# Reciprocal roots of the first block's norms: from VectorE's queue to GpSimd's

## The chip, the cores and the metric

The kernel runs on one core of a Trainium2 chip. A core has five engines that run side by side, each with its own queue of instructions in a fixed order: TensorE (matrix products, PE in the profile), VectorE (DVE), ScalarE (ACT), GpSimd (POOL) and SyncE (SP, which here only issues transfers). They wait for one another by semaphores. An instruction that has to wait holds up all that stand behind it in its engine's queue. The metric is the time of one execution on the device in microseconds, the median of several runs.

## The reference, cut to what matters

Two blocks are computed one after the other on 256 tokens of width 1024. The change touches the first block alone. It has two layers; the first also carries 256 context tokens along. Each layer normalizes its input, scales and shifts it by a modulation vector, multiplies by a wide matrix, and feeds the parts of the product to four branches: latent attention, a convolution, a Fourier mixing and a spatial gating.

```python
def _rmsnorm(x, g):
    y = x * lax.rsqrt(jnp.mean(x * x, axis=-1, keepdims=True) + RMS_EPS)
    return y * g

def _layernorm(x, g, b):
    mu = jnp.mean(x, axis=-1, keepdims=True)
    var = jnp.mean(jnp.square(x - mu), axis=-1, keepdims=True)
    return (x - mu) * lax.rsqrt(var + LN_EPS) * g + b
...
h = _rmsnorm(x, p["norm_g"]) * (1.0 + scale) + shift    # input of a layer
c_q = _rmsnorm(q_part, p["q_norm_g"])                   # latent attention, queries
c_kv = _rmsnorm(kv_part, p["kv_norm_g"])                # latent attention, keys and values
v = _layernorm(v, p["sgu_ln_g"], p["sgu_ln_b"])         # spatial gating
y = silu(_layernorm(y, p["conv_ln_g"], p["conv_ln_b"])) # convolution
```

Each of these has one reciprocal square root for each token, so one column of 128 numbers for a tile of 128 tokens. The second block has norms too; theirs are not touched.

## The kernel before, in words

Tokens lie in four tiles of 128 (t = 0, 1 are the tokens, t = 2, 3 the context), on the 128 partitions. All large products are made in three matmuls from a rounded high part and a remainder of each operand (hi and lo, whi and wlo): ScalarE casts a weight tile to whi and VectorE subtracts to get wlo, for 1024 columns at a time. Weights stream from memory through a few buffers (raw). The names in the profile are those of the tiles.

The order of the work is written by a planner in Python, `Sched`. It keeps a clock for each engine and runs generators: `main(t)` for the matmuls of a tile, and side generators for everything else (`mla`, `sgu`, `conv`, `fourier`, `modulate`, ...). `S.dve`, `S.act` and `S.pool` emit one instruction on VectorE, ScalarE or GpSimd and add its planned cost to the clock; a `Chain` carries the planned time of a dependent sequence. Nothing of it is on the chip: it only decides in which order instructions are emitted. The framework behind it then sets buffers and waits, and can place instructions of one engine that are ready ahead of others.

What the change and the prediction's steps touch:

- `rsqrt` (L372): a first guess from the bits of the number and three Newton steps, tiles rs_y, rs_h and rs_t; for one column 8 instructions, for more columns 11. All on VectorE, line L221 of the helper `S.dve`.
- `modulate` (L1293): between the two layers, once for each of the four tiles. The squares come from ScalarE (junk, ss), then the sum rw, the root, then xn = x times the root, one half on ScalarE and one half on VectorE; TensorE transposes xn, ScalarE applies the modulation (f) and casts (hhi), VectorE makes the remainder (hlo).
- `layernorm` (L1324), called by `sgu` for four tiles in the first layer and two in the second: statistics (bn, mv), rwl, the root, the shift lnb, and then ln on ScalarE.
- `mla` (L1575): squares on ScalarE (jq, jk), the sum ssm with a small constant, the root of two columns (queries and keys) or of one (`kv_only`, tiles 2 and 3 in the second layer). ScalarE uses it when it copies the products pkv and pq out of PSUM (qkf, V).
- `conv` (L1419): 31 taps of two multiply-adds each on VectorE (acc), spread between other work, and then a root of four or two columns.
- GpSimd's queue holds memsets (qkf, qz) and a few transfers.

Of the kernel before, what the change touches and what calls it, by code (L numbers as in the profile page):

```python
# [10 lines left out]
I32 = mybir.dt.int32  # L11
AF = mybir.ActivationFunctionType
ALU = mybir.AluOpType
# [6 lines left out]
EPS = 1e-6  # L20
# [73 lines left out]
LN_EPS = 1e-5  # L94
# [72 lines left out]
class Sched:  # L167
# [51 lines left out]
    def dve(self, ch, n, fn, *a, x=0.0, **k):  # L219
        self.issue("dve", ch, 0.07 + n * 0.00104 + x)  # L220
        ins = getattr(self.nc.vector, fn)(*a, **k)  # L221
        return ins

    def pool(self, ch, cost, fn, *a, **k):
        self.issue("pool", ch, cost)
        return getattr(self.nc.gpsimd, fn)(*a, **k)
# [142 lines left out]

def rsqrt(S, ch, pool, w, n, tag):  # L372

    y = pool.tile([P, n], F32, tag=tag + "y", name="rs_y", bufs=4)
    h = pool.tile([P, n], F32, tag=tag + "h", name="rs_h")
    t = pool.tile([P, n], F32, tag=tag + "t", name="rs_t")
    S.dve(ch, n, "tensor_scalar", y.bitcast(I32), w.bitcast(I32), -0.5, float(0x5F3759DF), op0=ALU.mult, op1=ALU.add)
    S.dve(ch, n, "tensor_scalar", h, w, -0.5, None, op0=ALU.mult)
    for _ in range(3):
        if n == 1:  # L380
            S.dve(ch, n, "scalar_tensor_tensor", t, y, h, y, op0=ALU.mult, op1=ALU.mult, x=0.06)
        else:
            S.dve(ch, n, "tensor_tensor", t, y, y, op=ALU.mult)
            S.dve(ch, n, "tensor_tensor", t, t, h, op=ALU.mult)
        S.dve(ch, n, "scalar_tensor_tensor", y, t, 1.5, y, op0=ALU.add, op1=ALU.mult)
    return y


class Second:
# [8 lines left out]
    def open(self, apool, src):  # L398

        self.ap = apool  # L400
        tab = apool.tile([P, src.shape[1]], F32, name="tab")
        if PADS[1]:
            apool.tile([P, PADS[1] // 4], F32, name="pad2")
        self.nc.gpsimd.dma_start(tab, src)
# [563 lines left out]
class First:  # L968
# [192 lines left out]
    def start(self):  # L1161
# [3 lines left out]
        self.ada = [self.p1.tile([P, 24, 2], F32, name=f"ada{l}") for l in range(2)]  # L1165
        self.p1.tile([P, PADS[2] // 4], F32, name="pad1")
        self.cbc = [self.s4([P, 1024], f"cbc{s}") for s in both]
# [125 lines left out]
    def modulate(self, t, l, x, ch, ss, ev):  # L1293

        S, s = self.S, t // 2
        new = self.hp.tile if t < 2 else self.p1.tile
        kw = (dict(tag="hhi"), dict(tag="hlo")) if t < 2 else (dict(tag="s4", bufs=S4),) * 2
        hi, lo = (new([P, KT, P], F32R, name=n, **k) for n, k in zip(("hhi", "hlo"), kw))
        w = self.small.tile([P, 1], F32, tag="rw", name="rw")
        S.dve(ch, 1, "scalar_tensor_tensor", w, ss[:, 0:1], EPS, ss[:, 1:2], op0=ALU.add, op1=ALU.add)  # L1300
        r = rsqrt(S, ch, self.small, w, 1, "r")
        xn = [self.normed(Chain(ch.t), x, r, n, n == 1) for n in range(2)]
        yield ch
        for n in range(2):
            for p in (0, 1):
                yield self.adaev[l, p, n]
            tp = self.psum("tp", "tpx")
            ch = S.chain()
            for k in range(4):
                self.tr(ch, tp[:, k * P:(k + 1) * P], xn[n][:, k * P:(k + 1) * P])  # L1310
            f = self.w2([P, 4, P], "f")
            for k in range(4):
                c = 4 * n + k
                S.act(ch, 128, "activation", f[:, k, :], tp[:, k * P:(k + 1) * P], AF.Identity,
                      scale=self.ada[l][:, 8 + c, s:s + 1], bias=self.ada[l][:, c, s:s + 1], x=0.15)
            h = slice(4 * n, 4 * n + 4)
            S.act(ch, 512, "copy", hi[:, h, :], f)
            S.dve(ch, 512, "tensor_sub", lo[:, h, :], f, hi[:, h, :].bitcast(F32))
            if n == 0:
                S.done(ev, ch)  # L1320
        self.hs[t] = lambda k: (hi[:, k, :], lo[:, k, :])


    def layernorm(self, ch, src, n):  # L1324

        S = self.S
        st = self.small.tile([P, 6], F32, tag="bn", name="bn")
        mv = self.small.tile([P, 2], F32, tag="mv", name="mv", bufs=4)
        S.dve(ch, n, "bn_stats", st, src)
        S.dve(ch, 6, "bn_aggr", mv, st)  # L1330
        w = self.small.tile([P, 1], F32, tag="rw", name="rwl")
        S.dve(ch, 1, "tensor_scalar", w, mv[:, 1:2], LN_EPS, None, op0=ALU.add)
        r = rsqrt(S, ch, self.small, w, 1, "r")
        b = self.small.tile([P, 1], F32, tag="lnb", name="lnb", bufs=4)
        S.dve(ch, 1, "scalar_tensor_tensor", b, mv[:, 0:1], -1.0, r, op0=ALU.mult, op1=ALU.mult)
        z = self.w2([P, 256], "ln")
        S.act(ch, 256, "activation", z, src, AF.Identity, scale=r, bias=b, x=0.15)
        return z
# [80 lines left out]
    def conv(self, l, streams):  # L1419
        nc, S = self.nc, self.S  # L1420
        for s in streams:
            for i in range(2):
                yield self.L[l].ev["glu", 2 * s + i]
        n = len(streams)
        sl = slice(streams[0], streams[-1] + 1)
        acc = self.p1.tile([P, 2, n, 256], F32, tag="acc", name="acc", bufs=1)
        acc = [acc[:, c] for c in range(2)]
        chs = [S.chain(), S.chain()]
        for j in range(31):
            for c in range(2):  # L1430
                src = self.glu[:, c, sl, j:j + 256]
                w = self.cw[l][:, c * 31 + j:c * 31 + j + 1]
                if j == 0:
                    S.dve(chs[c], 256 * n, "tensor_scalar", acc[c], src, w, self.col(l, "conv_b", c), op0=ALU.mult,
                          op1=ALU.add, x=0.12)
                else:
                    S.dve(chs[c], 256 * n, "scalar_tensor_tensor", acc[c], src, w, acc[c], op0=ALU.mult, op1=ALU.add, x=0.06)
            yield max(0.1, S.backlog("dve", 1.3) - CONV)
        ch = S.chain(*chs)
        yield ch  # L1440

        m = 2 * n
        mv = self.small.tile([P, 4, 2], F32, tag="mv4", name="mv4", bufs=1)[:, :m, :]
        ch, src = S.chain(), []
        for s in range(n):
            tp = self.psum(("tp", "ps")[s], "tpc")
            cs = S.chain()
            for i in range(2):
                for c in range(2):
                    self.tr(cs, tp[:, (2 * i + c) * P:(2 * i + c + 1) * P], acc[c][:, s, i * P:(i + 1) * P])  # L1450
            for i in range(2):
                st = self.small.tile([P, 6], F32, tag="bn", name="bn")
                src.append(tp[:, i * 256:(i + 1) * 256])
                S.dve(cs, 256, "bn_stats", st, src[-1])
                S.dve(cs, 6, "bn_aggr", mv[:, 2 * s + i, :], st)
            ch.t, ch.e = max(ch.t, cs.t), cs.e
        w = self.small.tile([P, 4], F32, tag="rw4", name="rw4c", bufs=1)[:, :m]
        S.dve(ch, 4, "tensor_scalar", w, mv[:, :, 1], LN_EPS, None, op0=ALU.add)
        r = rsqrt(S, ch, self.small, w, m, f"rc{m}")
        b = self.small.tile([P, 4], F32, tag="lnb4", name="lnb4", bufs=1)[:, :m]  # L1460
        S.dve(ch, 4, "scalar_tensor_tensor", b, mv[:, :, 0], -1.0, r, op0=ALU.mult, op1=ALU.mult)
        for i in range(m):
            z = self.w2([P, 256], "ln")
            cz = Chain(ch.t)
            S.act(cz, 256, "activation", z, src[i], AF.Identity, scale=r[:, i:i + 1], bias=b[:, i:i + 1], x=0.15)
            S.spawn(self.conv_out(l, 2 * streams[0] + i, z, cz))
# [108 lines left out]
    def mla(self, t, ps, kv_only=False):  # L1575
        nc, S, l = self.nc, self.S, self.l[t]
# [3 lines left out]
        ch = S.chain()  # L1580
        w = 160 if kv_only else 416
        p0 = 96 if kv_only else 0
        a = self.w2([P, 416], "mla")
        S.act(ch, w, "copy", a[:, :w], ps[:, p0:p0 + w])
        ss = self.small.tile([P, 2], F32, tag="ssm", name="ssm", bufs=4)
        if not kv_only:
# [4 lines left out]
        S.act(ch, 128, "activation", jk[:, :P], a[:, o:o + P], AF.Square, scale=math.sqrt(1.0 / 128), accum_out=ss[:, 1:2],  # L1591
              x=0.09)
        if kv_only:
            S.dve(ch, 1, "tensor_scalar", ss[:, 1:2], ss[:, 1:2], EPS, None, op0=ALU.add)
            r = rk = rsqrt(S, ch, self.small, ss[:, 1:2], 1, "r")
        else:
            S.dve(ch, 2, "tensor_tensor", ss, ss, self.eps2, op=ALU.add)
            r = rsqrt(S, ch, self.small, ss, 2, "r2")
            rk = r[:, 1:2]
        self.read(t)  # L1600
        yield ch
# [1 line left out]
        n = 1 if kv_only else 3  # L1603
# [38 lines left out]
        ch = S.chain(*([ck] + ([cq] if cq else [])))  # L1642
# [282 lines left out]


BANKS = 4
PADS = (1920, 0, 96)
TANH = (1,)
WX = (3,40,64)  # L1930
KEYP = 52
# [9 lines left out]
def build(tc, a, wst, widths, n1, tab, ident, cols, rows, lamp, out):  # L1941
    nc = tc.nc
    with ExitStack() as ctx:
# [3 lines left out]

        pool("pad", 1).tile([P, PADS[0] // 4], F32, name="pad")
        wp, hp, work, rawp, cp = pool("wp", WBUFS), pool("hp", 2), pool("work", 2), pool("rawp", RAWB), pool("const", 1)
# [80 lines left out]
```

## Time and profile before

| | |
|---|---|
| median of 3 runs | 1458.26 us (1457.76 to 1458.6) |
| the profiled execution's own time | 1456.91 us |
| span of its instructions | 1455.1 us |
| mean granted TensorE clock, as a share of 2.4 GHz | 0.993 |
| TensorE busy | 1404.0 us (96%) |
| VectorE busy | 986.8 us (68%) |
| ScalarE busy | 759.6 us (52%) |
| GpSimd busy | 30.3 us (2%), 47 instructions |

The profiled execution is one run; its own time is that of the whole execution, and its span goes from the first to the last instruction. Matmuls are pipelined, so that TensorE's busy time does not say that it ran at its peak. The first block takes the first 456 us.

### The profile page before, as it was taken

What the parts mean: (1) busy time and instruction counts of PE and PEld (TensorE: products, weight loads), DVE (VectorE), ACT (ScalarE), POOL (GpSimd) and SP (SyncE); (2) the same over time, 40 slices, a digit from 0 to 9 for tenths busy, and PEclk for the clock granted to TensorE, in tenths of its full rate; (3) what the DMA queues carried; (4) which work ended last, traced back from release to release, by engine and by line L of the source; (5) the groups of instructions that cost most, each with busy time, mean ns of one, the idle gap of its engine ahead of it and who ended that gap; (6) DMA issues with size and microseconds to landing.
All of it is one profiled execution on the core that took longest, in us unless ns stands there. A gap on an engine that the chain in (4) does not pass through costs nothing.

```text
span 1455.1 us, 19378 instructions
## 1 busy us (share of the span) xinstructions
PE 1404.0 (96%) x6950; PEld 1131.9 (78%) x6950; DVE 986.8 (68%) x2118; ACT 759.6 (52%) x1334; POOL 30.3 (2%) x47
## 2 busy tenths in 40 slices
PE   6999999899999999999999999999999999999997
PEld 6776777677877888877878888788888778788886
DVE  5898588779768555587886555675555878855554
ACT  4563443386466444467655444554445676554442
POOL 1000000010000000000000000000000000000000
PEclk9999999999999999999999999999999999999999
DMA  8731257543337565663446565565666544465651
GB/s 304 244 120 59 91 177 234 171 149 109 110 108 258 188 187 188 188 203 116 140 136 191 188 186 187 161 204 186 188 188 189 187 131 131 145 193 187 186 187 58
DMA packets 69089, 245.67 MB, mean 169 GB/s; under 512 B 7840, under 2 KB 8096, under 8 KB 68864
## 3 DMA queue, kind: packets, MB, share of 16 engines
q1 hardware_dynamic: 66384, 235.11, 50.9%
q0 software_dynamic: 2176, 8.79, 1.8%
q8 instruction: 55, 0.90, 0.2%
q10 hardware_dynamic: 432, 0.53, 0.1%
q14 instruction: 42, 0.34, 0.1%
HBM read 243.35 MB, written 1.05 MB: 168 GB/s over the span
## 4 chain that ended last, share of the span: by engine, by line
PE 79%; DVE 11%; ACT 4%; DMA 3%; issue 2%; SPq 0%; DVEq 0%; ACTq 0%
PE u L230 39%; PE y L230 18%; PE m L230 9%; DVE wlo L221 2%; PE tpg L234 1%; DMA ada<-in_ada_dram 1%; DVE adaj L221 1%; PE yo L230 1%; PE sc L230 1%; PE dft L230 1%; DVE acc L221 1%; PE tpp L234 1%; DMA raw<-in_wst_dram 1%; DVE rs_t L221 1%; PE av L230 1%
## 5 line engine op out<-in xcount | busy, mean ns | idle before, releaser
L221 DVE TENSOR_TENSOR wlo<-raw,whi 128x1024 fp32r<-128x1024 f32 (+1 forms) x380 | 458.9, 1211 | 341.3 <-ACT whi L216 340.6
L216 ACT CAST whi<-raw 128x1024 fp32r<-128x1024 f32 (+1 forms) x380 | 394.7, 1042 | 379.6 <-PE u L230 234.7
L230 PE MATMUL u<-whi,h_hi 128*128 128x512 f32 x704 | 281.2, 400 | 0.2 <-ACT h_hi L216 0.2
L230 PE MATMUL u<-whi,h_lo 128*128 128x512 f32 x704 | 275.1, 391 | 0.8 <-DVE h_lo L221 0.8
L230 PE MATMUL u<-wlo,h_hi 128*128 128x512 f32 x704 | 275.8, 392 | 0.0
L230 PE MATMUL y<-whi,g 128*128 128x512 f32 x704 | 218.5, 391 | 0.5 <-ACT g L216 0.5
L230 PEld LDWEIGHTS y<-whi,g 128*128 128x128 f32 x704 | 132.1, 188 | 28.8 <-ACT g L216 0.8
L230 PEld LDWEIGHTS u<-wlo,h_hi 128*128 128x128 f32 x704 | 132.2, 188 | 27.7
L230 PEld LDWEIGHTS u<-whi,h_lo 128*128 128x128 f32 x704 | 132.6, 188 | 27.1 <-DVE h_lo L221 2.3
L230 PEld LDWEIGHTS u<-whi,h_hi 128*128 128x128 f32 x704 | 132.3, 188 | 25.3 <-ACT h_hi L216 0.7
L230 PE MATMUL y<-wlo,g 128*128 128x512 f32 x352 | 137.5, 391 | 0.0
L230 PE MATMUL u<-whi,hhi 128*128 128x512 f32 (+2 forms) x256 | 98.6, 388 | 0.9 <-ACT whi L216 0.7
L230 PE MATMUL u<-wlo,hhi 128*128 128x512 f32 (+2 forms) x256 | 94.6, 374 | 2.7 <-DVE wlo L221 2.6
L230 PE MATMUL u<-whi,hlo 128*128 128x512 f32 (+2 forms) x256 | 94.8, 370 | 0.0
L230 PE MATMUL m<-whi,h_hi 128*128 128x512 f32 x192 | 79.1, 416 | 0.4 <-ACT h_hi L216 0.4
L221 DVE CUSTOM_DVE_ANT_0 adaj<-ada,cbc 128x1024 bf16<-128x1024 f32 x60 | 71.5, 1221 | 11.8 <-DMA ada<-in_ada_dram 11.1
L230 PEld LDWEIGHTS y<-wlo,g 128*128 128x128 f32 x352 | 66.1, 188 | 14.3
L230 PE MATMUL m<-wlo,h_hi 128*128 128x512 f32 x192 | 75.5, 395 | 0.0
L230 PE MATMUL m<-whi,h_lo 128*128 128x512 f32 x192 | 75.4, 394 | 0.0
L221 DVE SCALAR_TENSOR_TENSOR acc<-glu,cw,acc 128x512 f32<-128x512 f32 (+1 forms) x120 | 70.3, 613 | 0.0
L230 PEld LDWEIGHTS u<-wlo,hhi 128*128 128x128 f32 x256 | 48.3, 189 | 10.6 <-DVE wlo L221 4.1
L230 PEld LDWEIGHTS u<-whi,hhi 128*128 128x128 f32 x256 | 48.3, 189 | 8.4 <-issue 1.2
(303 smaller groups left out, 1941.9 us busy)
## 6 DMA issues: line engine op xcount, KB each, us to landing
raw<-in_wst_dram SPq DMA_DIRECT2D x376, 512.0 KB, 3.6
ada<-in_ada_dram SPq DMA_DIRECT2D x34, 512.0 KB, 4.0
grow<-in_rows_dram POOLq DMA_DIRECT2D x10, 512.0 KB, 5.1
adag<-in_adan_dram SPq DMA_DIRECT2D x8, 512.0 KB, 4.1
raw<-in_wst_dram SPq DMA_DIRECT2D x8, 416.0 KB, 4.0
ada<-in_adan_dram SPq DMA_DIRECT2D x6, 512.0 KB, 5.5
raw<-in_wst_dram SPq DMA_DIRECT2D x8, 256.0 KB, 2.6
tab<-in_tab_dram POOLq DMA_DIRECT2D x1, 1536.0 KB, 9.7
```

What stands on the lines that cost most here:

```text
L216: ins = getattr(self.nc.scalar, fn)(*a, **k)
L221: ins = getattr(self.nc.vector, fn)(*a, **k)
L230: self.nc.tensor.matmul(*a, **k)
L234: self.nc.tensor.transpose(out, in_, ident)
```

## The change

`rsqrt` gets the emitter of its instructions as an argument. With the new `S.tiny` they go to GpSimd, planned at 0.2 us each. GpSimd gets plain forms: a fused (a op b) op c of two tensors becomes two instructions. `modulate`, `layernorm` and `mla` pass `S.tiny`, and the few column instructions ahead of the root and behind it go the same way; the roots of the first start, of `conv` and of the second block stay on VectorE. The tag of the convolution's root is renamed so that it shares its buffers with others of the same width, and two unused pads in SBUF grow by 512 bytes a partition each.

```diff
+    def tiny(self, ch, n, fn, *a, **k):
+        return self.pool(ch, 0.2, fn, *a, **k)

-def rsqrt(S, ch, pool, w, n, tag):
+def rsqrt(S, ch, pool, w, n, tag, small=None):
+    small = small or S.dve
     y = pool.tile([P, n], F32, tag=tag + "y", name="rs_y", bufs=4)
...
-    S.dve(ch, n, "tensor_scalar", y.bitcast(I32), w.bitcast(I32), -0.5, float(0x5F3759DF), op0=ALU.mult, op1=ALU.add)
-    S.dve(ch, n, "tensor_scalar", h, w, -0.5, None, op0=ALU.mult)
+    small(ch, n, "tensor_scalar", y.bitcast(I32), w.bitcast(I32), -0.5, float(0x5F3759DF), op0=ALU.mult, op1=ALU.add)
+    small(ch, n, "tensor_scalar", h, w, -0.5, None, op0=ALU.mult)
     for _ in range(3):
-        if n == 1:
-            S.dve(ch, n, "scalar_tensor_tensor", t, y, h, y, op0=ALU.mult, op1=ALU.mult, x=0.06)
+        if n == 1 and small == S.dve:
+            small(ch, n, "scalar_tensor_tensor", t, y, h, y, op0=ALU.mult, op1=ALU.mult, x=0.06)
         else:
-            S.dve(ch, n, "tensor_tensor", t, y, y, op=ALU.mult)
-            S.dve(ch, n, "tensor_tensor", t, t, h, op=ALU.mult)
-        S.dve(ch, n, "scalar_tensor_tensor", y, t, 1.5, y, op0=ALU.add, op1=ALU.mult)
+            small(ch, n, "tensor_tensor", t, y, y, op=ALU.mult)
+            small(ch, n, "tensor_tensor", t, t, h, op=ALU.mult)
+        if small == S.dve:
+            small(ch, n, "scalar_tensor_tensor", y, t, 1.5, y, op0=ALU.add, op1=ALU.mult)
+        else:
+            small(ch, n, "tensor_scalar", t, t, 1.5, None, op0=ALU.add)
+            small(ch, n, "tensor_tensor", y, t, y, op=ALU.mult)

 # modulate
-        S.dve(ch, 1, "scalar_tensor_tensor", w, ss[:, 0:1], EPS, ss[:, 1:2], op0=ALU.add, op1=ALU.add)
-        r = rsqrt(S, ch, self.small, w, 1, "r")
+        S.tiny(ch, 1, "tensor_scalar", w, ss[:, 0:1], EPS, None, op0=ALU.add)
+        S.tiny(ch, 1, "tensor_tensor", w, w, ss[:, 1:2], op=ALU.add)
+        r = rsqrt(S, ch, self.small, w, 1, "r", S.tiny)

 # layernorm
-        S.dve(ch, 1, "tensor_scalar", w, mv[:, 1:2], LN_EPS, None, op0=ALU.add)
-        r = rsqrt(S, ch, self.small, w, 1, "r")
+        S.tiny(ch, 1, "tensor_scalar", w, mv[:, 1:2], LN_EPS, None, op0=ALU.add)
+        r = rsqrt(S, ch, self.small, w, 1, "r", S.tiny)
...
-        S.dve(ch, 1, "scalar_tensor_tensor", b, mv[:, 0:1], -1.0, r, op0=ALU.mult, op1=ALU.mult)
+        S.tiny(ch, 1, "tensor_tensor", b, mv[:, 0:1], r, op=ALU.mult)
+        S.tiny(ch, 1, "tensor_scalar", b, b, -1.0, None, op0=ALU.mult)

 # conv
-        r = rsqrt(S, ch, self.small, w, m, f"rc{m}")
+        r = rsqrt(S, ch, self.small, w, m, f"r{m}")

 # mla: the same for kv_only with one column
-            S.dve(ch, 2, "tensor_tensor", ss, ss, self.eps2, op=ALU.add)
-            r = rsqrt(S, ch, self.small, ss, 2, "r2")
+            S.tiny(ch, 2, "tensor_tensor", ss, ss, self.eps2, op=ALU.add)
+            r = rsqrt(S, ch, self.small, ss, 2, "r2", S.tiny)

-PADS = (1920, 0, 96)
+PADS = (1920, 512, 608)
```

## Rows read from the trace of the kernel before

**Rows 1.** The page: busy us (share); chain; a group (busy, mean ns).

```profile
PE 1404.0 (96%) x6950; PEld 1131.9 (78%) x6950; DVE 986.8 (68%) x2118; ACT 759.6 (52%) x1334; POOL 30.3 (2%) x47
...
PE 79%; DVE 11%; ACT 4%; DMA 3%; issue 2%; SPq 0%; DVEq 0%; ACTq 0%
...
L221 DVE TENSOR_TENSOR wlo<-raw,whi 128x1024 fp32r<-128x1024 f32 (+1 forms) x380 | 458.9, 1211 | 341.3 <-ACT whi L216 340.6
```

**Rows 2.** Busy us of three stretches of the first block (xinstructions).

```profile
84.00:150.00 66.00, 60.77 (x349) 43.88 (x347) 60.40 (x151) 30.72 (x73) 0.00 (x0) 0.95 0.23 75
...
276.00:320.00 44.00, 41.08 (x205) 33.33 (x204) 28.14 (x69) 29.73 (x64) 3.33 (x4) 1.00 0.35 115
...
320.00:360.00 40.00, 38.49 (x194) 29.81 (x193) 39.05 (x139) 29.70 (x67) 0.95 (x1) 1.00 0.46 152
```

**Rows 3.** Chain of waits by line, of 64:84, 84:150, 276:320, 320:352.

```profile
by line: PE u L230 35.1%; DVE wlo L221 12.1%; issue 10.5%; ACT cT L216 7.5%; DVE rs_t L221 7.0%; DVE acc L221 6.8%; DVE rot L221 4.7%; DVE rs_y L221 4.0%; ACT glu L216 2.7%; ACT mla L216 2.6%; ACT qkf L216 1.9%; ACT jk L216 1.5%; DVE ssm L2
...
by line: PE u L230 21.9%; DVE acc L221 18.1%; PE dft L230 18.0%; PE sc L230 9.8%; PE tpp L234 6.0%; PE sgum L230 5.2%; PE av L230 4.4%; PE fo L230 2.6%; issue 1.8%; ACT ln L216 1.7%; DVE wlo L221 1.7%; ACT p L216 1.7%; DVE bn L221 1.1%; DVE
...
by line: ACT f L216 25.5%; PE yo L230 12.4%; issue 9.6%; DVE wlo L221 8.0%; ACT hhi L216 6.9%; PE u L230 5.2%; ACT xn L216 5.0%; DVE rs_y L221 4.3%; DVE rs_t L221 4.3%; ACT junk L216 4.0%; ACT whi L216 3.9%; DVE x L221 3.2%; DVE upd L221 3.
...
by line: DVE wlo L221 14.7%; DVE acc L221 13.8%; DMA raw<-in_wst_dram 13.2%; PE tph L234 8.9%; issue 8.1%; PE pkv L230 6.2%; DVE rot L221 5.9%; DVE rs_t L221 5.3%; DVE rs_y L221 4.4%; PE u L230 4.4%; ACT whi L216 3.3%; DVE qkf L221 3.1%; PE
```

**Rows 4.** Timeline of VectorE, 283 to 300 us: start, us, what.

```profile
283.66 0.16 DVE L221 SCALAR_TENSOR_TENSOR rw<-ssx 128x1 f32<-128x1 f32 x1 [0.79 <-ACT junk L216]
...
285.45 0.48 DVE L221 TENSOR_SCALAR xn<-x,rs_y 128x512 f32<-128x512 f32 x1
...
294.64 0.16 DVE L221 SCALAR_TENSOR_TENSOR rw<-ssx 128x1 f32<-128x1 f32 x1 [0.97 <-ACT junk L216]
...
296.15 1.22 DVE L221 TENSOR_TENSOR wlo<-raw,whi 128x1024 fp32r<-128x1024 f32 x1
...
297.28 0.15 DVE L221 SCALAR_TENSOR_TENSOR rs_y<-rs_t,rs_y 128x1 f32<-128x1 f32 x1
...
299.75 0.15 DVE L221 SCALAR_TENSOR_TENSOR rs_y<-rs_t,rs_y 128x1 f32<-128x1 f32 x1
```

**Rows 5.** Timeline of VectorE, 92 to 99 us.

```profile
92.58 0.16 DVE L221 TENSOR_SCALAR rwl<-mv 128x1 f32<-128x1 f32 x1
...
93.43 0.75 DVE L221 SCALAR_TENSOR_TENSOR acc<-glu,cw,acc 128x512 f32<-128x512 f32 x1
...
94.09 0.23 DVE L221 SCALAR_TENSOR_TENSOR rs_t<-rs_y,rs_h 128x1 f32<-128x1 f32 x1
...
94.22 0.76 DVE L221 SCALAR_TENSOR_TENSOR acc<-glu,cw,acc 128x512 f32<-128x512 f32 x1
...
98.65 0.18 DVE L221 SCALAR_TENSOR_TENSOR lnb<-mv,rs_y 128x1 f32<-128x1 f32 x1
```

**Rows 6.** Timeline of ScalarE, 285 to 335 us.

```profile
285.45 0.72 ACT L216 ACTIVATE xn<-x,rs_y 128x512 f32<-128x512 f32 x1 [1.82 <-DVE rs_y L221]
...
289.97 0.72 ACT L216 ACTIVATE xn<-x,rs_y 128x512 f32<-128x512 f32 x1 [1.89 <-DVE rs_y L221]
...
290.60 1.83 ACT L216 ACTIVATE f<-tpx,ada 128x128 f32<-128x128 f32 x5
...
334.48 0.47 ACT L216 ACTIVATE qkf<-pkv,rs_y 128x256 f32<-128x256 f32 x1 [0.54 <-PE pkv L230]
```

**Rows 7.** Timeline of GpSimd, 3 to 326 us.

```profile
3.47 0.12 POOL L1014 MEMSET eps<- 128x1 f32 x1
...
295.22 1.84 POOL L226 MEMSET qkf<- 128x1024 f32 x2 [0.57 <-PE yo L230]
...
325.14 0.95 POOL L226 MEMSET qkf<- 128x1024 f32 x1 [14.33 <-PE kv L230]
```

**Rows 8.** Timeline of VectorE, 325 to 326 us.

```profile
325.49 0.62 DVE L221 TENSOR_SCALAR rs_h<-ssm 128x2 f32<-128x2 f32 x1
```

**Rows 9.** Waits, 0 to 456 us: who <- whom: us, times, longest.

```profile
ACT ln L216 <- DVE lnb L221: 29.2, 7, 9.5
```

More of the change, by code (lines that the diff above doesn't have):

```diff
@@ L1593, in mla @@
         if kv_only:
-            S.dve(ch, 1, "tensor_scalar", ss[:, 1:2], ss[:, 1:2], EPS, None, op0=ALU.add)
-            r = rk = rsqrt(S, ch, self.small, ss[:, 1:2], 1, "r")
-        else:
-            S.dve(ch, 2, "tensor_tensor", ss, ss, self.eps2, op=ALU.add)
-            r = rsqrt(S, ch, self.small, ss, 2, "r2")
+            S.tiny(ch, 1, "tensor_scalar", ss[:, 1:2], ss[:, 1:2], EPS, None, op0=ALU.add)
+            r = rk = rsqrt(S, ch, self.small, ss[:, 1:2], 1, "r", S.tiny)
+        else:
+            S.tiny(ch, 2, "tensor_tensor", ss, ss, self.eps2, op=ALU.add)
+            r = rsqrt(S, ch, self.small, ss, 2, "r2", S.tiny)
             rk = r[:, 1:2]
```

## The prediction

> **What bounds the kernel now.** I read the page first. TensorE sets the end over the whole run: it holds 79% of the chain that ended last, VectorE 11%, and VectorE is busy 68% of the span against 2% for GpSimd [rows 1]. The change touches only the first block, which runs from the start to about 456 us, so the average over the span says little; I went on to the busy times by stretch, and then to the chain of waits of the same stretches. From 84 to 150 us VectorE is busy 60.4 of 66 us, from 320 to 360 us 39.05 of 40, from 276 to 320 us only 28.1 of 44 [rows 2]. In the first two of these VectorE also stands in the chain: with its large instructions, that is the weight remainders (wlo), the convolution (acc) and the rotations (rot, qkf), it holds 23.6% of 64 to 84 us, 19.8% of 84 to 150 us and 37.5% of 320 to 352 us [rows 3]. The instructions that the change moves stand in it as rs_t and rs_y: 11.0% of 20 us, 8.6% of 44 us and 9.7% of 32 us, that is 2.2, 3.8 and 3.1 us [rows 3]. So the moved work is on the path that sets the end, but a small part of it.
>
> **The change part by part.** It takes reciprocal roots off VectorE at 18 places: four times in `modulate` (9 instructions each), six times in `layernorm` for the spatial gating (10 each), six times in `mla` with two columns (12 each) and twice with one (9 each): 186 instructions. GpSimd gets 16, 17, 15 and 15 for the same places, because a fused multiply-add-multiply becomes two instructions: 286. None of them feeds a DMA, and each depends on the one before.
>
> *Price of one.* On VectorE a chain with nothing between, that of `modulate` for the first tile, runs from 283.66 to the start of xn at 285.45: 9 instructions in 1.79 us, 0.2 us each [rows 4]. When other work is between, an instruction of the chain costs VectorE itself less: in the gating of the first tile one of them stands between two acc instructions, and the chain lasts from 92.58 to 98.83 us, 6.2 us for 10 [rows 5]. GpSimd has run nothing that reads SBUF. The nearest row is a memset of one column, 0.12 us [rows 7]: that is the lower bound of an instruction of the chain. The upper bound is an instruction that has to let one of VectorE's pass each time: 0.12 plus the 0.66 us from one acc to the next, 0.78 us, or 0.12 plus 1.13 us behind a weight remainder (from 296.15 to the start of the next instruction at 297.28), 1.25 us [rows 4, 5]. For a free GpSimd I take 0.3 us, an estimate from the memset's 0.12 and VectorE's step of 0.2 for reading what was just written; it is nearer to the lower end because the row is one of the same engine and width.
>
> *Whether the two engines block each other.* There is one row that shows it: while GpSimd's memset of 0.95 us ran from 325.14 to 326.09, VectorE's rs_h of two columns, started at 325.49, took 0.62 us, where other instructions of such chains take 0.15 to 0.23, and ended at 326.11 [rows 4, 5, 7, 8]. A weight remainder beside another pair of memsets, at 296.15, took 1.22 us, about the mean of all 380, 1.21 [rows 1, 4, 7]. The Trainium skill (SBUF — State Buffer, section "Who interferes with whom") states that the pair of ports that the two engines share is an exclusive lock, and that a VectorE instruction with two SBUF inputs collides with a GpSimd instruction that reads SBUF, not with one that only writes. By that rule both rows come out as they did, and nearly all large VectorE instructions of these stretches would collide with the new ones; the row of the memset cannot show that part, since a memset reads nothing.
>
> *(1) VectorE relieved.* Of the moved instructions 2.2 us and 3.1 us stand in the chain in the two stretches without `modulate`, and in the gating chain some 0.9 us (10 instructions between acc, up to 0.13 us each from one start to the next, as for rs_t at 94.09; 0.09 on average taken) [rows 3, 5]: 6.2 us together. What comes next behind them is TensorE's own work, so not all of it is won. Bounds 0 and -6.2; I take half, -3.
>
> *(2) VectorE held up by GpSimd.* 128 of the new instructions fall into 64 to 150 us and 94 into 320 to 360 us. If each holds VectorE for 0.12 us, that is 15.4 and 11.3 us of VectorE; the shares of the chain that VectorE's large instructions have there (21% and 37.5% [rows 3]) make it 3.2 + 4.2 = 7.4 us. Bounds 0 and +7.4; half, +3.7, since at times VectorE waits anyway and reads PSUM in part of its work.
>
> *(3) The four chains of `modulate`.* Here nothing covers them well: ScalarE waits 1.82 and 1.89 us for r of the first two tiles [rows 6], and behind the second of these waits stand the f instructions of the first tile, which make layer 1's h. On GpSimd 16 instructions at 0.3 us are 4.8 us against 1.79: +3.0 us for each of the first two. TensorE has output matmuls of the other tiles to do meanwhile, and ScalarE may be given f of the first tile ahead of the second xn; I count one of the two, +3.0. The third chain takes 5.1 us now (294.64 to 299.75) because weight remainders lie between [rows 4]; GpSimd would need 4.8 us, and two to three of its instructions would be stretched by a remainder, 6 to 8 us. For the third and fourth together I take +1.5. Sum +4.5; bounds 0 (all covered) and +14 (16 steps of 0.12 + one remainder for the late two, nothing covered for the early two).
>
> *(4) The six chains of the gating.* ScalarE waits for their result or for that of the convolution seven times, 29.2 us in all, up to 9.5 us, with other tiles' work behind it in its queue [rows 9]. The first takes 6.2 us. On a free GpSimd 17 instructions are 5.1 us; if each lets one acc pass, 17 x 0.78 = 13.3 us. The middle, 9.2, is 3 us more. Three of the six touch the chain of waits, and there ScalarE's share is small (ln 1.7% of 84 to 150 us [rows 3]): I take +1, bounds -3 and +9.
>
> *(5) The chains of `mla`.* 15 instructions are 4.5 to 18 us; for layer 1's first tile r is needed at 334.48 us, where ScalarE waits for a matmul (pkv) and not for r [rows 6]. Taken as 0; without that cover some 7 us, once.
>
> *(6) The rest.* New positions in GpSimd's queue: ahead of or behind the memsets of qkf (0.95 us each, one of which waited for a matmul until 325.14 [rows 7]); a chain behind it would start 1.5 us late, in the stretch of (5), which has that cover. The renamed tags of the convolution's root share their buffers with chains that have long ended; the pads give back the bytes that these tiles leave. Both 0. The planner in the kernel counts the new instructions as longer, so the order of everything else may move; I put nothing on that but width.
>
> Sum: -3 + 3.7 + 4.5 + 1 = +6.2 us. The profiled execution took 1456.9 us, 1.35 us under the median of the runs, so it becomes 1463.1, and the median of the runs about **1464.5 us**.
>
> **The rivals.** *VectorE's relief wins (faster).* Place: 64 to 150 and 320 to 352 us. If a step of a GpSimd chain stays under about 0.36 us also while VectorE is busy (6.2 us by 17 steps), the gating gets no slower and ScalarE waits less: -6.2 for (1), 0 for (2), some -3 for (4), and with f of one tile run in the wait for the next, +1.5 for (3): about -7.7 us, 1450.5 us. For it speaks how full VectorE is [rows 2] and that no row shows a reading GpSimd instruction blocked; against it that `modulate`, where VectorE has time, loses in any case, since 16 steps would have to be under 0.11 us to match 1.79.
>
> *Each step waits a whole VectorE instruction (much slower).* If the lock goes to VectorE whenever it has work, (2) is 0 but (4) is +9 and (3) +14: about +20 to +25 us with (1), 1480 us. For it speaks the 0.62 us row [rows 8], against it that blocking there lasted no longer than one instruction.
>
> *Nothing measurable.* TensorE holds most of the chain; if it has other tiles' matmuls wherever a root is late, (3) shrinks to about 1.5 and cancels (1): 1458 us.
>
> The Trainium skill (GPSIMD Engine Reference, section "Engine selection") advises against GpSimd for elementwise arithmetic, at about half VectorE's speed for two inputs. By that the sum would be on the slow side too; at one column the price is per instruction and not per element, and no run here shows it yet.
>
> **How the numbers follow.** Forecast as in the sum 45%; relief wins 32%; nothing measurable 15%; whole waits 8%. Range 1449 to 1482 us: from the relief rival's end (1450.5 less the spread of the order) to the case of whole waits; the forecast's own range is 1459 to 1472. About 0.2%, 2.9 us, is what a measurement of this kernel can tell from no change. Faster by more than that: the relief rival, 0.32. Slower: forecast and whole waits, less 0.02 for a forecast that ends under +2.9 us: 0.51. Within: 0.17.
>
> **What would show it.** In the profile of the changed kernel: GpSimd with some 333 instructions; a free chain of `modulate` at 283 us with a step of 0.25 to 0.35 us, xn 3 us later; in the gating steps between 0.3 and 0.8 us, locked to the ends of acc; acc and wlo with a longer mean. If steps during acc are as short as during `modulate`, there is no blocking, (2) falls and the relief rival gains. If ScalarE's wait for xn is gone because f stands in front of it, (3) falls. The prediction is wrong outright if the order of the whole block moves, with transfers or table loads at other places, by more than the sum.

## The result, and the profile after

The changed kernel takes 1496.3 us (median of four runs, 1495.3 to 1497.0) against 1458.0 before: a ratio of 1.0265, interval 1.0247 to 1.0283. It is slower by 38.3 us, where the prediction had +6 and its range ended at 1482. The profiled execution has a span of 1494.4 us.

The page of the changed kernel, busy times and chain, beside [rows 1]:

```profile
PE 1408.4 (94%) x6950; PEld 1136.7 (76%) x6950; DVE 967.9 (65%) x1932; ACT 756.9 (51%) x1332; POOL 115.2 (8%) x333
...
PE 77%; DVE 7%; POOL 6%; issue 4%; DMA 3%; ACT 2%; SPq 0%; DVEq 0%; ACTq 0%; POOLq 0%
```

VectorE lost its 186 instructions and 18.9 us of work, GpSimd gained 286. The stretches of [rows 2] in the changed kernel:

```profile
84.00:150.00 66.00, 54.64 (x335) 41.62 (x334) 49.28 (x96) 25.04 (x63) 21.68 (x61) 0.92 0.13 43
276.00:320.00 44.00, 27.79 (x110) 21.95 (x111) 22.42 (x31) 16.06 (x31) 11.65 (x53) 0.81 0.41 126
320.00:360.00 40.00, 38.02 (x200) 32.51 (x199) 27.31 (x47) 28.86 (x66) 14.80 (x29) 0.96 0.50 156
```

From 84 to 150 us VectorE was busy for 11 us less (60.4 to 49.3). That is not relief alone: for 12.4 us of this stretch it now waits for ln. TensorE did not gain either: it was busy for 54.6 us instead of 60.8. From 276 to 320 us TensorE lost 13 us more, and its granted clock stood at 0.81 on average, between its levels of 1.2 and 2.4 GHz, where it was 1.00 before. Waits of the first 500 us in the changed kernel (who <- whom: us, times, longest), beside [rows 9]:

```profile
DVE ln L221 <- ACT ln L216: 34.0, 6, 10.1
ACT ln L216 <- POOL lnb L230: 27.7, 6, 7.4
DVE xn L221 <- POOL rs_y L230: 17.4, 4, 5.2
ACT qkf L216 <- POOL qkf L230: 15.2, 2, 9.3
ACT xn L216 <- POOL rs_y L230: 15.2, 4, 4.5
```

ScalarE's wait for the gating's result is a little longer than before: 27.7 us in six waits against 22.9 us in five (of the seven in [rows 9], two with 6.3 us are for the convolution's ln). The first and the third line are new: VectorE, which used to compute the roots, now stands still for them, 51 us in all. `modulate` shows how. The first chain on GpSimd, from the instruction that waits for the last sum to the last one:

```profile
294.46 0.19 POOL L230 TENSOR_TENSOR rw<-rw,ssx 128x1 f32<-128x1 f32 x1 [22.24 <-ACT junk L216]
...
298.57 0.19 POOL L230 TENSOR_TENSOR rs_y<-rs_t,rs_y 128x1 f32<-128x1 f32 x1
```

VectorE at the same time:

```profile
298.79 0.49 DVE L221 TENSOR_SCALAR xn<-x,rs_y 128x512 f32<-128x512 f32 x1 [5.23 <-POOL rs_y L230]
299.19 0.68 DVE L221 TENSOR_TENSOR upd<-yo,gate 128x512 f32<-128x512 f32 x1
...
305.82 0.49 DVE L221 TENSOR_SCALAR xn<-x,rs_y 128x512 f32<-128x512 f32 x1 [5.21 <-POOL rs_y L230]
306.22 0.69 DVE L221 TENSOR_TENSOR upd<-yo,gate 128x512 f32<-128x512 f32 x1
```

A free step is 0.2 us long and starts 0.28 us after the one before, as estimated. But xn of one tile stands in VectorE's queue ahead of upd of the next, and upd starts the next tile's norm: the first two tiles' xn, 4.5 us apart before [rows 6], are now 7.0 us apart.

### The profile page after: what moved, and what is told of

Its sections match the earlier page's. It is cut to its first block, busy times and chain, and to the rows that moved or that the text cites. A ratio compares the mean times of both kernels' runs of the same rounds, so it can differ in the third digit from the quotient of the medians.

```text
span 1494.4 us, 19487 instructions
## 1 busy us (share of the span) xinstructions
PE 1408.4 (94%) x6950; PEld 1136.7 (76%) x6950; DVE 967.9 (65%) x1932; ACT 756.9 (51%) x1332; POOL 115.2 (8%) x333
## 4 chain that ended last, share of the span: by engine, by line
PE 77%; DVE 7%; POOL 6%; issue 4%; DMA 3%; ACT 2%; SPq 0%; DVEq 0%; ACTq 0%; POOLq 0%
PE u L234 38%; PE y L234 17%; PE m L234 9%; POOL rs_t L230 3%; PE tpg L238 1%; DMA ada<-in_ada_dram 1%; DVE adaj L221 1%; PE yo L234 1%; POOL rs_y L230 1%; PE sc L234 1%; PE tpp L238 1%; DMA ada<-in_adan_dram 1%; PE av L234 1%; DVE wlo L221 1%; DMA raw<-in_wst_dram 1%
## 5 line engine op out<-in xcount | busy, mean ns | idle before, releaser
L234 PEld LDWEIGHTS u<-wlo,h_hi 128*128 128x128 f32 x704 | 132.2, 188 | 27.7
L221 DVE SCALAR_TENSOR_TENSOR acc<-glu,cw,acc 128x512 f32<-128x512 f32 (+1 forms) x120 | 67.3, 609 | 0.0
L446 POOL DMA_DIRECT2D grow<-in_rows_dram x10 | 5.3, 531 | 649.2 <-DVE rw L221 638.9
```

Source lines behind the costliest of these rows:

```text
L234: self.nc.tensor.matmul(*a, **k)
L446: self.nc.gpsimd.dma_start(g, self.rows[l, j:j + 1, :].to_broadcast([P, D]))
```

## The experiments

**Order or engine?** The planner was given new costs, so the order of much other work moved too. The first run keeps the new plan and computes on VectorE, the second keeps the old plan and computes on GpSimd. (A plan is kept nearly, not exactly: of the 6950 matmuls of a profile about 1% and 2% stand elsewhere in the order than in their models; between the two kernels it is 11%.) Of the two edits only the new emitter is shown; the rest sets the forms of the steps.

```diff
 def tiny(self, ch, steps, fn, *a, **k):       # first run
-    return self.pool(ch, 0.2, fn, *a, **k)
+    for _ in range(steps):
+        self.issue("pool", ch, 0.2)
+    return getattr(self.nc.vector, fn)(*a, **k)
 def tiny(self, ch, n, fn, *a, x=0.0, plan=True, **k):       # second run
-    return self.pool(ch, 0.2, fn, *a, **k)
+    if plan:
+        self.issue("dve", ch, 0.07 + n * 0.00104 + x)
+    return getattr(self.nc.gpsimd, fn)(*a, **k)
```

> The planner is given the changed kernel's costs (one GpSimd instruction of 0.2 us for every step), so nearly all other work is issued in the order of the changed kernel, but the roots run on VectorE in the forms of the kernel before. Theory A (late chains: the steps on GpSimd and their one queue cost the time): 1453 to 1466 us. Theory B (the new order of the block costs it): 1485 to 1497 us. Theory C (VectorE's large instructions are slowed by GpSimd): 1453 to 1466 us, as A.

> The converse: the planner is given the costs of the kernel before, so nearly all other work keeps the order of the kernel before, and the roots run on GpSimd. Theory A: 1483 to 1500 us, about the changed kernel's 1496. Theory B: 1456 to 1470 us, with modulate's 3 us each for the first two tiles the only loss. Theory C: 1475 to 1500 us, and then the mean of acc at 128 partitions x 512 elements and of the weight remainders is longer than before by the loss divided by their count in the first block; under A it is longer by less than 3%.

Measured: 1457.9 us (ratio 1.0004, 0.9995 to 1.0014) and 1500.0 us (1.0295, 1.0278 to 1.0311). The new order costs nothing; theory B is out. VectorE's large instructions of the first block, grouped by form (count | busy us, mean ns), before and then in the changed kernel:

```profile
L221 DVE TENSOR_TENSOR wlo<-raw,whi 128x1024 fp32r<-128x1024 f32 x51 | 62.1, 1221 | 12.8 <-ACT whi L216 12.7
L221 DVE SCALAR_TENSOR_TENSOR acc<-glu,cw,acc 128x512 f32<-128x512 f32 x60 | 43.7, 748 | 0.0
```

```profile
L221 DVE TENSOR_TENSOR wlo<-raw,whi 128x1024 fp32r<-128x1024 f32 x52 | 63.0, 1221 | 12.3 <-ACT whi L216 11.9
L221 DVE SCALAR_TENSOR_TENSOR acc<-glu,cw,acc 128x512 f32<-128x512 f32 x60 | 41.9, 740 | 0.0
```

In the second run the means are 1222 and 742 ns. GpSimd does not make VectorE's large instructions longer; theory C is out as well.

**Which part?** Each of the three places alone on GpSimd, the other two as before (the diff is the change's own, cut to `modulate`, to `layernorm`, to `mla`).

> Only the four roots of modulate go to GpSimd. Theory A: each of the four tiles comes 2.5 to 3 us later, one after the other, since VectorE's half of xn stands ahead of the next tile's update: +10 to +16 us, 1468 to 1474 us. The recorded prediction's term (3): +4.5 us, 1462.5 us. Theory B: whatever the order does, 1455 to 1465.

> Only the six roots of the gating's layernorm go to GpSimd. Theory A: without mla's chains in the same queue they are stretched behind acc only (17 steps of some 0.6 us, 10 us against 6), and ScalarE waits for some of them: +3 to +10 us, 1461 to 1468 us. The recorded prediction's terms (1), (2) and (4) for this part: about -1 to +3 us. A relief of VectorE that wins: 1452 to 1455 us.

> Only the eight roots of mla go to GpSimd. The parts of modulate and of the gating cost 9.8 and 23.8 us alone, the whole change 38 to 39 us. If the parts only add up, mla gives the remaining 4 to 6 us: 1462 to 1464 us. If the one queue matters in itself (roots of several tiles and the memsets of qkf one behind the other), mla alone costs more, +8 to +20 us, 1466 to 1478 us, and the whole is less than the sum. The recorded prediction's term (5): 0, or some +7 us without its cover.

Measured: 1467.5 us (+9.8; 1.0058 to 1.0092), 1481.5 us (+23.8; 1.0152 to 1.0182), 1473.4 us (+15.5; 1.0091 to 1.0122). The sum is 49, more than the 38 of the whole: the parts' delays overlap in part. `modulate` ends just under the 1468 to 1474 us expected, `mla` inside the range of the one queue. The gating costs far more than any theory said, and its first chain is hardly longer than before: from rwl at 92.92 to the end of lnb at 99.51 us, 6.6 us against 6.25 from rwl to the end of lnb in [rows 5]. VectorE before, from the input of the chain (mv) to the first instruction behind ln, and then in that run:

```profile
91.86 0.18 DVE L221 BATCH_NORM_AGGREGATE mv<-bn 128x2 f32<-128x6 f32 x1
...
99.46 0.43 DVE L221 TENSOR_TENSOR ln<-ln,rows 128x256 f32<-128x256 f32 x1
```

```profile
92.64 0.18 DVE L221 BATCH_NORM_AGGREGATE mv<-bn 128x2 f32<-128x6 f32 x1
92.73 3.38 DVE L221 SCALAR_TENSOR_TENSOR acc<-glu,cw,acc 128x512 f32<-128x512 f32 x5
100.15 0.42 DVE L221 TENSOR_TENSOR ln<-ln,rows 128x256 f32<-128x256 f32 x1 [4.04 <-ACT ln L216]
```

Before, acc and the chain alternated on VectorE [rows 5]: ten acc ran between the chain's input and the product behind ln. Now five stand there, and then VectorE waits 4.04 us. Over six tiles that is 26.1 us. The chain's 6.6 us rest on this standstill: its first five steps, beside acc, took 0.55 to 0.67 us each, the other twelve 0.19 to 0.21.

**modulate: is it xn's place in the queue?**

```diff
-xn = [self.normed(Chain(ch.t), x, r, n, n == 1) for n in range(2)]
 yield ch
+cx = [Chain(ch.t) for n in range(2)]
+xn = [self.normed(cx[n], x, r, n, n == 1) for n in range(2)]
+yield cx[0]
```

> As the run with modulate alone, but xn is issued only when the planner has the root done, so that VectorE's half of it need not stand ahead of the next tile's update. Theory A1: VectorE's wait of 3 to 5 us in front of each tile's update goes, tiles overlap, and the time falls by 5 us or more, to 1456 to 1462 us. Theory A2 (TensorE waits for the first root in any case): 1463 to 1470 us.

Measured: 1458.7 us (1.0005, 0.9995 to 1.0015). Against the kernel before, the whole 9.8 us went. The chains on GpSimd are still there; most of VectorE's wait for them is not (17.3 us over four waits without the delay, here 4.6 over two):

```profile
DVE xn L221 <- POOL rs_y L230: 4.6, 2, 2.6
```

**The gating: which queue is held up?** First only VectorE's two instructions behind ln, a product and a sum (below: the products), are issued later, by a `yield ch` in front of them; then 4 us later still (`yield 4.0`); the second also together with `modulate`.

> As the run with the gating alone, but the two products of VectorE behind ln are issued only when the planner has the root and ln done, so that more convolution stands ahead of them in VectorE's queue. Theory A1 (VectorE stands idle behind a product that waits for GpSimd's chain: 26 us over six tiles, and that is the loss): VectorE's waits for ln fall to under 10 us in all, and the time to 1455 to 1467 us. Theory A2 (the chain's lateness itself holds up TensorE; VectorE's idle time costs nothing): no change, 1476 to 1484 us. A GpSimd chain lasts about as long as the chain on VectorE did (6.4 us against 6.2), which speaks for A1.

> As the run with the gating's ln issued later, but 4 us later still, so that 11 instead of 5 instructions acc stand ahead of the first tile's product. Theory A1 (VectorE's idle time is the loss): VectorE's waits for ln fall to under 8 us and the time to 1456 to 1466 us. Theory A3 (a chain on GpSimd gets on by about one step for each two-input instruction of VectorE, 0.66 us, and at its free 0.28 us only while VectorE stands idle): with VectorE kept busy the first chain takes 8 to 11 us instead of 6.4, and the time stays at 1468 to 1478 us.

> Roots of modulate and of the gating on GpSimd with xn and ln issued later as in the two runs before, those of mla on VectorE as in the kernel before. Theory A1: 1454 to 1464 us. Theory A3: modulate's part is free, the gating's is not, 1468 to 1480 us.

Measured: 1473.0 us (1.0085 to 1.012), 1486.7 us (1.0194 to 1.0224) and 1484.1 us (1.0174 to 1.0209). The first lies between its two theories: VectorE's waits for ln fell only to 19.6 us. The other two are worse than either theory allowed. In the second run VectorE no longer waits for ln at the first tile, and the chain takes 8.1 us. Its ScalarE and its VectorE:

```profile
99.86 0.56 ACT L216 ACTIVATE ln<-u,lnb,rs_y 128x256 f32<-128x256 f32 x1 [6.28 <-POOL lnb L230]
...
102.18 0.29 ACT L216 COPY adarow<-adaps 128x128 f32<-128x128 f32 x1
```

```profile
91.52 6.01 DVE L221 SCALAR_TENSOR_TENSOR acc<-glu,cw,acc 128x512 f32<-128x512 f32 x9
103.27 0.16 DVE L221 TENSOR_TENSOR ada<-adaps,cols 128x4 f32<-128x4 f32 x1 [5.74 <-PE adaps L234]
```

ScalarE's ln waits 6.28 us for lnb, with copies of other parts behind it; TensorE needs one of those (adarow), and VectorE needs TensorE (adaps). So two queues stood behind the root, and only one had been cleared. The next run issues ln itself later as well; beside it one with the length of the chain cut and all other order kept.

```diff
         S.tiny(ch, 1, "tensor_scalar", b, b, -1.0, None, op0=ALU.mult)
+        yield ch
         z = self.w2([P, 256], "ln")
...
-    for _ in range(3):
+    for i in range(3):                          # the other run: one iteration
+        if small != S.dve and i:
+            for _ in range(4):
+                S.issue("pool", ch, 0.2)
+            continue
```

> As the run with the gating alone, but ln itself on ScalarE and its products on VectorE are both issued only when the planner has the root done. In the run with the products 4 us later VectorE stopped waiting for ln at the first tile, but then waited 5.7 us for TensorE, which waited for ScalarE, whose ln stood ahead of other tiles' softmax and copies and waited for the root (35.5 us over six tiles). Theory A4 (both in-order queues are held up, and the loss goes only when neither stands behind the root): ScalarE's waits for lnb fall below 20 us and the time to 1457 to 1466 us. Rival A3 (the stretched chain itself is late for TensorE): 1470 to 1485 us.

> As the run with the gating alone, with the same order of all other work, but of the three iterations of the root only the first is computed (the other two are left out): 9 GpSimd instructions a chain instead of 17, some 3.8 us instead of 6.4. If the lateness of the chain is what costs: VectorE's and ScalarE's waits for it fall by about 2.5 us a tile, and of the 24 us at least 12 go: 1459 to 1470 us. If the handing over between engines costs, or the order of the other work: 1474 to 1482 us.

Measured: 1456.3 us (0.9988, 0.9979 to 0.9997) and 1462.0 us (1.003, 1.0016 to 1.0043). With both queues cleared the 24 us are gone (the first run ends just under the 1457 to 1466 us of theory A4). The waits of ScalarE and VectorE for the chain, in the run of the gating alone and then with ln issued later:

```profile
ACT ln L216 <- POOL lnb L230: 33.9, 6, 7.8
DVE ln L221 <- ACT ln L216: 26.1, 6, 6.0
```

```profile
DVE ln L221 <- ACT ln L216: 4.3, 2, 3.1
ACT ln L216 <- POOL lnb L230: 1.3, 1, 1.3
```

And this although GpSimd's first chain became longer, 8.1 us (92.66 to 100.80):

```profile
92.66 0.63 POOL L230 TENSOR_SCALAR rwl<-mv 128x1 f32<-128x1 f32 x1 [85.55 <-DVE mv L221]
...
100.59 0.21 POOL L230 TENSOR_SCALAR lnb<-lnb 128x1 f32<-128x1 f32 x1
```

84 to 150 us of the gating alone, without and with ln issued later (two runs, a fence each):

```profile
84.00:150.00 66.00, 57.60 (x347) 42.84 (x345) 48.31 (x101) 26.62 (x65) 16.04 (x52) 0.95 0.15 51
```

```profile
84.00:150.00 66.00, 60.43 (x371) 45.78 (x370) 55.74 (x112) 32.21 (x77) 22.25 (x47) 0.95 0.20 66
```

VectorE and ScalarE do 7.4 and 5.6 us more work in the same 66 us, with the chains on GpSimd in both. The shortened chain (3.5 us at the first tile) takes 19 of the 24 us away: lateness costs as long as the queues stand behind it.

**mla: queue of roots, or the memset?** In the run with `mla` alone GpSimd takes the third and fourth tile's roots one after the other, step by step beside acc, and the memsets of qkf come behind them. GpSimd, then ScalarE:

```profile
94.72 0.65 POOL L230 TENSOR_TENSOR rs_t<-rs_y 128x2 f32<-128x2 f32 x1
...
97.63 1.84 POOL L230 MEMSET qkf<- 128x1024 f32 x2
```

```profile
98.61 0.47 ACT L216 ACTIVATE qkf<-pkv,rs_y 128x256 f32<-128x256 f32 x1 [7.76 <-POOL qkf L230]
```

So one run moves that memset in the changed kernel (`nc.vector.memset`, planned as before), another takes only the odd tiles' roots to GpSimd (`S.tiny if t % 2 else S.dve`).

> The changed kernel with the memset of qkf on VectorE in place of GpSimd, so that ScalarE's qkf instructions no longer wait for a memset that stands behind other tiles' roots. If these waits (15.2 us in all, longest 9.3) hold up the end: 1480 to 1491 us. If they lie beside the wait for the roots themselves, or VectorE's eight memsets cost as much: 1492 to 1500 us.

> Of mla's eight roots only those of the odd tiles (four of eight) go to GpSimd. mla alone cost 15.5 us. If each root costs by itself, by its later result: about half, +6 to +9 us, 1464 to 1467 us. If the queue is what costs (roots arrive every 2 to 4 us and one takes 4 to 10 us, so the third and fourth wait for the first two): under +4 us, 1457 to 1462 us.

Measured: 1499.5 us (against 1496.3 with the memset on GpSimd: nothing gained) and 1462.6 us (+5.4; 1.0025 to 1.0054). In the changed kernel the memset is not the limit by itself: without it ScalarE's wait for lnb grew from 27.7 to 40.5 us. Whether it is one where the other queues are cleared was not tried. Half the roots cost a third of the 15.5 us, between the two answers expected.

**Is the engine worth anything, or the order?** The kernel before with the delays, on VectorE (both; xn only; the products behind ln only), and the change with xn, ln and the products issued later, whole and without `mla`. The delays of the gating are not the same: on VectorE the products alone come 4 us later, on GpSimd ln and the products wait for the planned end of the root.

> The kernel before, all roots on VectorE, with the same two delays of xn and ln: shows what the delays do by themselves. All theories: 1454 to 1462 us.

> The kernel before, all roots on VectorE, with only xn of modulate issued later. With both delays it took 1447.7 us, 9.5 less than before. If xn makes the gain: 1447 to 1452 us. If ln makes it: 1455 to 1460 us.

> The kernel before, all roots on VectorE, with only the products behind ln issued later. If ln makes the gain of the run with both: 1447 to 1452 us. If xn makes it: 1455 to 1460 us.

> The whole change, with xn, ln and ln's products issued only when the planner has the root done. Theory A4 with the queue of mla: modulate's and the gating's share of the loss goes, mla's stays: 1466 to 1475 us. If mla's share too came only from what stood behind the gating's ln: 1455 to 1463 us. If the three parts together fill GpSimd's queue so that each is late again: 1480 to 1496 us.

> Roots of modulate and of the gating on GpSimd with xn, ln and ln's products issued later, those of mla on VectorE. Theory A4: both parts are free, and what is gained from the later xn comes on top: 1452 to 1458 us. With the roots on VectorE and like delays it took 1447.7 us: if GpSimd relieved VectorE, 1440 to 1447 us.

Measured, in that order: 1447.7 us (0.9941, 0.9921 to 0.996), 1454.3 (0.9978), 1450.9 (0.9955), 1464.1 (1.0046, 1.0031 to 1.0061) and 1447.6 (0.994, 0.9919 to 0.9962). The first was not expected by any theory (1454 to 1462 us); the second, the fourth and the fifth lie between their answers.

On VectorE the two delays give 2.9 and 6.3 us, together 9.5; with those roots on GpSimd, in an order of its own, it is 9.6. Both versions beat the kernel before by 0.6%. So the order gives what is gained, and no gain from relieving VectorE is seen. Where the edit is the same, GpSimd is slower: with xn alone issued later the ratio is 1.0005 on GpSimd and 0.9978 on VectorE, some 4 us, and with the products 4 us later it is 1.0209 and 0.9955. The order of the last run was not tried with all roots on VectorE, so what the engine costs or gives in that order is not shown.

With `mla` on GpSimd as well it takes 16.5 us more (1464.1 less 1447.6), about as much as `mla` alone. That loss is seen from 320 to 360 us, whole and then without `mla`:

```profile
320.00:360.00 40.00, 29.60 (x142) 22.14 (x141) 30.70 (x73) 19.88 (x50) 34.98 (x86) 0.91 0.35 115
```

```profile
320.00:360.00 40.00, 39.90 (x201) 30.46 (x200) 40.00 (x133) 28.28 (x64) 13.61 (x34) 1.00 0.37 121
```

GpSimd is occupied for 35 of 40 us (time in which a step waits for VectorE counted in), and TensorE, VectorE and ScalarE each lose 8 to 10. Here GpSimd is the engine the others wait for: in the chain of waits of this stretch, whole (shares of 40 us; most of the piece of issue lies ahead of them):

```profile
by line: POOL rs_t L230 54.6%; issue 52.7%; POOL rs_y L230 15.2%; POOL qkf L230 6.7%; POOL rs_h L230 4.6%; POOL rwl L230 3.2%; POOL ssm L230 2.9%; POOL lnb L230 1.7%; POOLq L230 0.2%
```

## Why the prediction was wrong

The step that failed is the one that (3) and (4) share: they priced a moved chain by its own length, less what covers it, and left out what stands behind the chain's consumers in the queues of VectorE and ScalarE. The gating alone cost 23.8 us, against an outer bound of +9. Beside it (5), taken as 0 and as some 7 us without its cover, cost 15.5: it left out that the chains share one queue.

- **Price of a step**: right. 0.28 us free against 0.3; 0.54 to 0.78 us beside acc of 512 columns, inside the bounds. Above them beside several remainders: 3.81 us, see the last section.
- **(1) and (2)**, relief and hold-up of VectorE, -3 and +3.7: (2) came out near 0, acc and wlo kept their means. Of (1) nothing is seen: the best runs with GpSimd and with VectorE take the same time (1447.6 and 1447.7 us), though not in the same order, so no run sets it apart. The row of 0.62 us [rows 8] was read as VectorE held up by a memset; the line behind the bullets shows that acc, begun during that memset, took its usual 0.48 us, so the work behind it was not.
- **(3) modulate**, +4.5: measured +9.8 alone. The chain's length was right (4.8 us foreseen, 4.3, 4.3, 5.0 and 4.5 measured; 6 to 8 had been set down for the last two), the cover was not. The step counted ScalarE's xn and the f behind it; it did not ask what stands behind VectorE's half of xn, the next tile's upd. So VectorE stood still at all four tiles, one after the other, for 17.3 us. With xn issued later nothing is lost against the kernel before, and some 4 us against the same edit with the roots on VectorE. The bound of +14 does not follow from the steps in its bracket.
- **(4) The gating**, +1, at most +9: measured +23.8 alone. This is the largest failure. The step took the price of the move as the change in the chain's length, and that hardly changed (6.6 us against 6.25, and 8.1 where VectorE was kept busy). The cost lay where the step did not look: a chain on VectorE is filled with VectorE's own other work, while a chain elsewhere leaves VectorE's and ScalarE's consumers (the products, ln) standing at the head of in-order queues. Shown by clearing the queues: a longer chain, no loss.
- **(5) mla**, taken as 0: measured +15.5 alone, 16.5 on top of the mended rest. The step looked at one result that was not waited for and priced each chain by itself. Its chains share one queue that takes 4 to 11 us for each, while they arrive 2 to 4 us apart. How much of the 16 us is the queue, how much the steps stretched beside VectorE, and how much the memsets behind them stays open: the two runs on it do not separate these.
- **(6)** The planner's order, put at nothing without a reason: it came out so (1457.9 us). The memsets: the step asked what a chain behind a memset loses, 1.5 us. The runs show the reverse, memsets behind the chains, and ScalarE waited up to 9.3 us for one; moving them gained nothing in the changed kernel.
- **The rivals**: of "each step waits a whole VectorE instruction" the mechanism is in the trace and the consequence is not; chains of 8.1 us cost nothing once nothing stood behind them. Relief did not win.

VectorE before, beside the memset of [rows 7] that ends at 326.09:

```profile
325.63 0.48 DVE L221 SCALAR_TENSOR_TENSOR acc<-glu,cw,acc 128x256 f32<-128x256 f32 x1
```

## What to carry to other kernels

Before moving a chain of small instructions to an idle engine, list who consumes its result and what stands behind that consumer in its queue; move the consumer back with it, or the engine that was to be relieved will idle instead. Then add up the target's single queue: arrivals against the time it takes for each, at the price beside a busy VectorE. And try the order alone on the old engine: here it gave 9.5 us, as much as the best run with roots on GpSimd.

## What the runs showed of the hardware

A GpSimd step can be held up by more than one instruction of VectorE. In the changed kernel, GpSimd and VectorE:

```profile
353.44 3.81 POOL L230 TENSOR_TENSOR rs_t<-rs_t,rs_h 128x2 f32<-128x2 f32 x1
```

```profile
353.70 3.49 DVE L221 TENSOR_TENSOR wlo<-raw,whi 128x1024 fp32r<-128x1024 f32 x3
```

The step ends at 357.25, the third remainder at 357.19: it got no turn between the three. VectorE meanwhile loses nothing (1221 ns each, as before). It is not always so. A few microseconds earlier eleven acc follow one another without a gap, and GpSimd's steps come through between them, most of them 0.31 to 0.43 us long:

```profile
347.42 4.44 DVE L221 SCALAR_TENSOR_TENSOR acc<-glu,cw,acc 128x256 f32<-128x256 f32 x11
```

```profile
349.54 0.39 POOL L230 TENSOR_TENSOR ssm<-ssm,eps 128x2 f32<-128x2 f32 x1
349.89 0.43 POOL L230 TENSOR_TENSOR rs_t<-rs_y 128x2 f32<-128x2 f32 x1
```

Between two remainders a step came through as well: of the two from 307.55 to 309.90 us the first ended at about 308.8, one step at 308.82, and the next, begun at 308.90, ended at 309.95. What decides whether a step gets a turn is open.

The Trainium skill (SBUF — State Buffer, section "Who interferes with whom") calls the port pair that the two engines share an exclusive lock, and says that a VectorE instruction with two SBUF inputs contends with a GpSimd instruction that reads SBUF. The trace agrees: the steps were blocked beside such instructions, for 3.81 us at most in the changed kernel.

A step on one or two columns is 0.18 to 0.23 us when free, and in a single chain the next one starts 0.27 to 0.30 us after it; 16 of them took 4.3 us where VectorE's nine took 1.79 [rows 4].
